# First block of a two-block network on one core: filter spectra moved among the modulation tiles, other modulation kinds moved later, GpSimd arithmetic moved to VectorE, hyena yields made finer

## The chip, the cores and the metric

One core of one Trainium2 chip runs the whole program in one launch. The metric is the device time of one execution in microseconds (us); smaller is better. Five engines work side by side, each through its own queue in order: PE (TensorE: matmuls and transposes), DVE (VectorE), ACT (ScalarE), POOL (GpSimd) and SP, which here only issues transfers from HBM. Float32 weights are used as a pair "high + low" of reduced-precision halves, so that one product takes three matmuls.

## The reference, cut to what matters

The network has two blocks on 256 tokens of width 1024. Only the mixer of the first block is touched:

```python
ada_x = jnp.split(s_lat @ w_ada[l] + b_ada[l], 6, axis=-1)      # six "kinds" of modulation
hx = modulate(rmsnorm(x, norm_mix_g[l]), ada_x[0], ada_x[1])    # kinds 0 and 1
yx, _ = token_mixer(hx, *mix_params, rows, GRID_W, ctx_state)
x = x + ada_x[2][:, None, :] * yx                               # kind 2
hx2 = modulate(rmsnorm(x, norm_ffn_g[l]), ada_x[3], ada_x[4])   # kinds 3 and 4
x = x + ada_x[5][:, None, :] * expert_choice_ffn(...)           # kind 5

def token_mixer(h, ...):
    p = h @ w_in + b_in
    y_a = hyena_branch(p[..., :ML_START], ...)    # 3 projections of 512; z = x_n * longconv(z, filter_n), twice
    y_b, state = mlstm_branch(...)                # q, k, v, o and gates; q, k, v of the context too
    g_a, g_b = jnp.split(jax.nn.sigmoid(p[..., MERGE_START:]), 2, axis=-1)
    return (g_a * (y_a @ w_branch_hy) + g_b * (y_b @ w_branch_ml)) @ w_out, state
```

The two filters of the hyena branch come from a small network of the position (two sines, then `f_w3`, times a decay); a long convolution is a product of spectra.

## The kernel before, in words

`phase_a` writes the first block's mixer, `experts` the expert network, `phase_c` the second block. The order on each engine is laid down at compile time by a list planner: an instruction written earlier has the higher priority, an estimated cost says when it is ready, and ready instructions of lower priority fill gaps. So each engine's order is fixed, but is not the order of the source, and what is late on the chip blocks what stands behind it on its engine. Generators (`filters`, `ada_rest`, `hyena`, `gates`) are advanced with `next` to spread their work over the projections.

**Weights.** Every tile of 1 MB is loaded by SP into one of four `raw` buffers, and `half` turns each of its two halves into high (ACT, line 258) and low (a subtraction, line 259, on DVE or on the engine that `sub` names) in one of four `whl` buffers. `fm` then multiplies (line 255, "mm" tiles in the trace).

**Modulation.** Kinds 0 and 1 are needed first: `ada_tile` loads eight 1 MB tiles and runs four small matmuls on each (line 392). In this loop PE's order is forced to be the order written (`chained`). `ada_close` adds the bias and transposes. The other kinds (`ada_rest`, order 3, 4, 2, 5) take four steps each: one 1 MB tile into a `raw` buffer and two passes over 128x1024 on DVE (lines 423, 425); the last step of a kind adds small matmuls with `ones`.

**Filters.** `filters` yields eight times: after each sine (1, 2), after each half of the two parities (3 to 6; after 4 and 6 the sums and differences `sd` of lines 514, 515), and after each of two spectra `K` in tiles G and H (7, 8), which need the transform table FT from `filter_loads(2)`. Here five steps are taken by the end of tile 3 of the modulation, 6 and 7 after the first hyena projection, 8 after the second.

**Then**: `modT` transposes and modulates x (tiles C, D); six hyena tiles `w_hy`, each followed by `conv` (two DVE passes, lines 618, 619, per 128 columns); in between `modT` of the context (E, F); `hyena` with a spectrum, products with K (lines 808 to 813), sums (816 to 819) and an inverse, twice; gates; `w_k`, `w_v`, `w_q`, `w_o`, and the mLSTM among the eight merge tiles `w_mg`; then `w_br`, `w_out` and the router. The sixteen steps of `ada_rest` go with the last four `w_hy`, the two each of `w_k`, `w_v`, `w_q`, `w_o`, and the first four `w_mg`. The expert weights go through a ring of 18 buffers, filled in order as the mixer frees them; the second round begins when the first expert has used the first.

Of the kernel before, what the change touches and what calls it, by code (L numbers as in the profile page):

```python
# [16 lines left out]
P = 128  # L17
# [210 lines left out]
class Builder:  # L228
# [253 lines left out]
    def filters(self):  # L482

        nc, I, ap = self.nc, self.I, self.ap
        zT, w1, w2, w3, dec, sk = self.fl
        h1, h2 = self.Q[:64, 3, :T], self.Q[:, 3, T:]
        ps = self.psum()
        self.mm(ps[:64, :T], w1, zT, True, True)
        self.sin(h1, ps[:64, :T], self.pfc("fb1")[:64])
        yield  # L490
        ps = self.psum()
        self.mm(ps[:, :T], w2, h1, True, True)
        self.sin(h2, ps[:, :T], self.pfc("fb2"))
        yield

        sd = [self.tl(ap, [P, 2, 2, 512], tag=x) for x in "EF"]
        hv = h2.rearrange("r (m two) -> r two m", two=2)
        for par in range(2):
            h = {}
            for di in range(2):  # L500
                ps = [self.psum(), self.psum()]
                for o in range(2):
                    r = slice(64 * o, 64 * o + 64)
                    self.mm(ps[o], hv[r, par], w3[r, di * 512:(di + 1) * 512], True, True)
                for o in range(2):
                    h[o, di] = self.tl(ap, [P, 512], tag="m2")
                    nc.vector.tensor_mul(h[o, di], ps[o], dec[:, par])
                if di == 0:
                    yield
            for o in range(2):  # L510
                if par == 0:
                    nc.vector.tensor_add(h[o, 0][0:1, :], h[o, 0][0:1, :], sk[:, o])
                    nc.vector.memset(h[o, 1][0:1, :], 0.0)
                nc.gpsimd.tensor_add(sd[o][:, 0, par], h[o, 0], h[o, 1])
                nc.gpsimd.tensor_sub(sd[o][:, 1, par], h[o, 1], h[o, 0])
            yield
        self.K = []
        for o in range(2):
            K = self.tl(ap, [P, 2, 2, 512], tag="GH"[o])
            self.spectrum(K, lambda ri, par: sd[o][:, ri, par])  # L520
            self.K.append(K)
            yield
# [275 lines left out]
    def hyena(self, z0, p1, p2):  # L798

        nc, ap = self.nc, self.ap  # L800
        z = z0
        for o in range(2):
            K = self.K[o]
            U = self.Q.rearrange("p (r s) n -> p r s n", r=2)
            self.spectrum(U, lambda ri, par: z[:, par])
            Y = self.tl(ap, [P, 2, 2, 512], tag="A")
            m = [self.op[:, :1024].rearrange("p (s n) -> p s n", s=2), self.tl(ap, [P, 2, 512], tag="S")]
            nc.vector.tensor_mul(Y[:, 0], U[:, 0], K[:, 0])
            nc.vector.tensor_mul(m[0], U[:, 1], K[:, 1])
            nc.gpsimd.tensor_add(Y[:, 0], Y[:, 0], m[0])  # L810
            nc.vector.tensor_mul(Y[:, 1], U[:, 0], K[:, 1])
            nc.vector.tensor_mul(m[1], U[:, 1], K[:, 0])
            nc.vector.tensor_sub(Y[:, 1], Y[:, 1], m[1])

            Z = U
            nc.vector.tensor_sub(Z[:, 0, 1], Y[:, 1, 0], Y[:, 1, 1])
            nc.vector.tensor_add(Z[:, 1, 1], Y[:, 1, 0], Y[:, 1, 1])
            nc.vector.tensor_add(Z[:, 0, 0], Y[:, 0, 0], Y[:, 0, 1])
            nc.vector.tensor_sub(Z[:, 1, 0], Y[:, 0, 0], Y[:, 0, 1])
            yield  # L820
            if o == 0:
                z = p1
                for par in range(2):
                    ps = self.psum()
                    for ri in (1, 0):
                        self.mm(ps, self.idft[:, par, ri], Z[:, par, ri], ri == 1, ri == 0)
                    nc.vector.tensor_mul(z[:, par], ps, p1[:, par])
            else:
                yy = self.tl(ap, [P, 2, 4, T], F32R, tag="G")
                yh, yl = yy[:, 0], yy[:, 1]  # L830
                for c in range(4):
                    ps = self.psum()
                    for par in range(2):
                        for ri in (1, 0):
                            self.mm(ps[:, par * P:(par + 1) * P], Z[:, par, ri, c * P:(c + 1) * P], self.idft[:, par, ri], ri == 1, ri == 0)
                    y = self.tl(ap, [P, T], tag="s1")
                    by = lambda v: v.rearrange("p (m two) -> p two m", two=2)
                    nc.vector.tensor_mul(by(y), ps[:, :T].rearrange("p (two m) -> p two m", two=2), by(p2[:, c]))
                    self.split(y, yh[:, c], yl[:, c])
                self.ya = yh, yl  # L840
# [10 lines left out]
    def phase_a(self):  # L851
        nc, tc, I = self.nc, self.tc, self.I
        with ExitStack() as es:
# [16 lines left out]
            with self.chained(mybir.EngineType.PE):  # L870
                for kc in range(KC):
                    if kc == 5:
                        xn = self.normed(I["x"], "A")
                    self.ada_tile(kc)
                    if kc == 0:
                        self.filter_loads(1)
                    if kc < 4:
                        next(fil)
            hy = [self.weights(I["w_hy"][0])]
            self.filter_loads(2)  # L880
            cn = self.normed(I["ctx"], "B")
            fm0 = self.ada_close()
            self.iota = self.tl(ap, [P, 32], tag="iota")
            nc.scalar.dma_start(self.iota, I["t_iota"])
# [6 lines left out]
            pfc = self.pfc  # L891
            taps = lambda nm, j, n: [pfc(nm, i * n + j) for i in range(3)]

            parts = []
            zt = self.tl(ap, [P, 2, 2, 512], tag="B")
            z8 = self.tl(self.cst, [P, 2, 4, T], tag="X")
            for p_ in range(3):
                z = z8[:, p_] if p_ < 2 else self.op[:, 1032:2056].rearrange("p (c n) -> p c n", c=4)
                for j in range(2):
                    w = hy.pop() if hy else self.weights(I["w_hy"][2 * p_ + j], sub=(None, nc.gpsimd))  # L900
                    if p_ > 0:
                        next(rest)
                    for c in range(2):
                        n = 2 * j + c
                        ps = self.psum("mm")
                        self.fm(ps[:, :T], w, c, xT)
                        self.conv(z[:, n], ps[:, :T], pfc("b_hy", 4 * p_ + n), taps("hyw", 4 * p_ + n, 12), 4)
                if p_ < 2:
                    next(fil)
                if p_ == 0:  # L910
                    next(fil)
                if p_ == 0:
                    cT = self.modT(cn, gs[:, 1], fm0[:, 1, 0:8], "EF", nc.gpsimd)
                parts.append(self.to_tm(z, zt[:, p_]) if p_ < 2 else z)
            hyena = self.hyena(*parts)
            next(hyena)
            gates = self.gates(xT, cT)
            next(gates)
            qo = self.tl(self.cst, [P, 2, 4, T], tag="X")
# [1 line left out]
            k = self.tl(ap, [P, 4, T], tag="J")  # L921
            kc = q
            for j in range(2):
                w = self.weights(I["w_k"][j], sub=(None, nc.gpsimd))
                next(rest)
                for c in range(2):
                    ps = self.psum("mm")
                    self.fm(ps[:, :T], w, c, cT)
                    self.fm(ps[:, T:], w, c, xT)
                    n = 2 * j + c  # L930
                    self.conv(kc[:, n], ps[:, :T], pfc("b_k", n), taps("mlw", 4 + n, 8), 1, AF.Silu)
                    self.conv(k[:, n], ps[:, T:], pfc("b_k", n), taps("mlw", 4 + n, 8), 4, AF.Silu)
                next(hyena, None)
                next(gates)
            ya = self.ya
            bv = self.tl(ap, [P, 512], tag="m2")
# [3 lines left out]
            for a in (v, vc):  # L940
                nc.gpsimd.memset(a[:, :, :, 128:129], 1.0)
            for j in range(2):
                w = self.weights(I["w_v"][j], sub=(None, nc.gpsimd))
                next(rest)
                for a, src in ((vc, cT), (v, xT)):
                    ps = self.mm2()
# [5 lines left out]
            C0 = self.mlstm_state(kc, vc)  # L952
            self.dump("C0", C0)
            for j in range(2):
                w = self.weights(I["w_q"][j], sub=(None, nc.gpsimd))
                next(rest)
                for c in range(2):
                    n = 2 * j + c
                    ps = self.psum("mm")
                    self.fm(ps[:, :T], w, c, xT)  # L960
                    self.conv(q[:, n], ps[:, :T], pfc("b_q", n), taps("mlw", n, 8), 4, AF.Silu)
            for j in range(2):
                w = self.weights(I["w_o"][j], sub=(None, nc.gpsimd))
                next(rest)
                for c in range(2):
                    n = 2 * j + c
# [10 lines left out]
            rows = self.bias_rows()  # L977
            for j in range(8):
                w = self.weights(I["w_mg"][j])
                if j < 4:  # L980
                    next(rest)
                elif j % 2 == 0:
                    next(rows)
                for c in range(2):
                    n = 2 * j + c
# [752 lines left out]
```

## Time and profile before

| | |
|---|---|
| median of 3 runs | 2452.0 us (2451.36 to 2458.77) |
| profiled execution, its own time | 2461.75 us |
| its span, first to last instruction | 2460.0 us |
| PE / DVE / ACT / POOL busy | 2092.1 / 1003.3 / 734.4 / 90.9 us |
| share of the critical chain, PE / DMA / DVE | 52% / 39% / 6% |

Times within the trace are counted from the span's start. The mixer of the first block takes the first 370 us, the experts go on to about 1240 us, the second block takes the rest. In a timeline the columns are start, duration, engine, line, operation, tiles (written <- read), shapes, count; what stands in brackets is the idle time of the engine just before and what ended it.

### The profile page before, as it was taken

Reading aid. Unit: us, or ns where it says so; the run is one execution under the profiler, and the core shown is the slowest. Engines: PE = TensorE matmul, PEld = TensorE weight load, DVE = VectorE, ACT = ScalarE, POOL = GpSimd, SP = SyncE. Lnnn points to the kernel's source line nnn. Section 1 sums busy time; section 2 is a strip of 40 time slices with the busy share of each in tenths; the row PEclk is TensorE's granted clock in tenths of the full one; section 3 lists DMA queues with packets and bytes.
Section 4 is the critical chain, followed back from the end, with each engine's and each line's share of the span. In section 5 each row is a group of like instructions: output and inputs, shape, how many; then the busy total and the mean of one; then the engine's idle time right before and its main releaser. Section 6 shows DMA issues by size and latency. Waiting matters only on the chain.

```text
span 2460.0 us, 35219 instructions
## 1 busy us (share of the span) xinstructions
PE 2092.1 (85%) x15084; PEld 1515.0 (62%) x15084; DVE 1003.3 (41%) x1494; ACT 734.4 (30%) x1110; POOL 90.9 (4%) x82
## 2 busy tenths in 40 slices
PE   6889987686667666766668999999999999999998
PEld 3778882021111101110117999999999999999998
DVE  5886660000000000000005666656555566657555
ACT  3435631000000000000003644444443554444442
POOL 3321000000000000000000000000000000000000
PEclk8989989798779877987778999999999999999999
DMA  8536579999999999999997445555555545555553
GB/s 309 196 126 221 210 280 378 421 420 420 421 420 421 421 420 421 421 420 421 420 404 262 165 145 177 184 189 187 181 199 194 170 143 179 168 195 181 192 178 107
DMA packets 109079, 675.73 MB, mean 275 GB/s; under 512 B 12245, under 2 KB 20534, under 8 KB 35323
## 3 DMA queue, kind: packets, MB, share of 16 engines
q1 hardware_dynamic: 97226, 657.20, 69.4%
q10 hardware_dynamic: 9952, 10.24, 1.5%
q0 software_dynamic: 1744, 6.04, 0.8%
q8 instruction: 118, 1.93, 0.3%
q14 instruction: 39, 0.31, 0.0%
HBM read 672.36 MB, written 1.08 MB: 274 GB/s over the span
## 4 chain that ended last, share of the span: by engine, by line
PE 52%; DMA 39%; DVE 6%; ACT 1%; issue 1%; POOL 1%; SPq 0%; POOLq 0%; ACTq 0%; DVEq 0%
PE mm L255 46%; DMA raw<-in_w_e 8%; DMA whl<-in_w_e 7%; PE ax L255 4%; DMA A<-in_w_e 2%; DMA acc<-in_w_e 2%; DMA F<-in_w_e 2%; DMA B<-in_w_e 2%; DMA OP<-in_w_e 2%; DMA C<-in_w_e 2%; DMA Q<-in_w_e 2%; DMA H<-in_w_e 2%; PE ax L252 2%; DMA V<-in_w_e 1%; DMA FT<-in_w_e 1%; DMA G<-in_w_e 1%
## 5 line engine op out<-in xcount | busy, mean ns | idle before, releaser
L255 PE MATMUL mm<-C,whl 128*128 128x256 f32 (+1 forms) x4072 | 739.1, 282 | 6.9 <-DVE whl L259 6.9
L259 DVE TENSOR_TENSOR whl<-raw,whl 128x1024 fp32r<-128x1024 f32 (+2 forms) x410 | 494.6, 1210 | 373.3 <-ACT whl L258 372.0
L255 PEld LDWEIGHTS mm<-C,whl 128*128 128x128 f32 (+1 forms) x4072 | 629.0, 189 | 12.8 <-DVE whl L259 7.7
L255 PE MATMUL mm<-D,whl 128*128 128x256 f32 (+1 forms) x2040 | 571.5, 280 | 0.8 <-DVE D L573 0.8
L258 ACT CAST whl<-raw 128x1024 fp32r<-128x1024 f32 (+1 forms) x423 | 435.8, 1035 | 411.6 <-PE mm L255 341.4
L255 PEld LDWEIGHTS mm<-D,whl 128*128 128x128 f32 (+1 forms) x2040 | 384.0, 188 | 4.4 <-issue 3.3
L1188 DVE TENSOR_TENSOR m<-mm,m 128x512 f32<-128x512 f32 x16 | 11.1, 692 | 571.5 <-PE mm L255 571.5
L1187 ACT ACTIVATE m<-mm 128x512 f32<-128x512 f32 x16 | 9.6, 597 | 750.6 <-PE mm L255 750.6
L255 PE MATMUL mm<-whl,C 128*128 128x256 f32 x768 | 141.1, 287 | 1.2 <-ACT whl L258 1.2
L1223 DVE TENSOR_TENSOR S<-mm,J 128x512 f32<-128x512 f32 (+1 forms) x9 | 5.4, 628 | 304.4 <-PE mm L255 304.4
L255 PE MATMUL mm<-raw,N 128*32 128x512 f32 x448 | 86.3, 862 | 46.9 <-DMA raw<-in_w_e 46.9
L255 PE MATMUL mm<-whl,BH 128*128 128x256 f32 x704 | 125.0, 281 | 0.0
L255 PEld LDWEIGHTS mm<-whl,C 128*128 128x128 f32 x768 | 119.6, 192 | 5.5 <-ACT whl L258 2.9
L255 PE MATMUL mm<-whl,N 128*32 128x512 f32 x432 | 73.8, 769 | 44.9 <-DMA whl<-in_w_e 44.8
L255 PE MATMUL mm<-whl,D 128*128 128x256 f32 x384 | 108.7, 283 | 0.0
L255 PEld LDWEIGHTS mm<-whl,BH 128*128 128x128 f32 x704 | 108.0, 188 | 0.0
L255 PE MATMUL mm<-whl,BL 128*128 128x256 f32 x352 | 98.9, 281 | 0.0
L255 PE MATMUL mm<-BH,whl 128*128 128x256 f32 x512 | 91.2, 281 | 0.0
L255 PEld LDWEIGHTS mm<-raw,N 128*32 128x32 f32 x448 | 10.9, 126 | 115.1 <-DMA raw<-in_w_e 108.5
L255 PE MATMUL mm<-whl,E 128*32 128x512 f32 (+2 forms) x304 | 65.8, 580 | 15.9 <-DMA whl<-in_w_e 15.9
L255 PEld LDWEIGHTS mm<-BH,whl 128*128 128x128 f32 x512 | 78.7, 188 | 0.0
L255 PEld LDWEIGHTS mm<-whl,N 128*32 128x32 f32 x432 | 10.1, 120 | 107.2 <-DMA whl<-in_w_e 97.8
(449 smaller groups left out, 2644.2 us busy)
## 6 DMA issues: line engine op xcount, KB each, us to landing
raw<-in_w_e SPq DMA_DIRECT2D x84, 1024.0 KB, 19.8
whl<-in_w_e SPq DMA_DIRECT2D x82, 1024.0 KB, 19.8
raw<-in_w_r SPq DMA_DIRECT2D x48, 1024.0 KB, 5.0
raw<-in_w_gu SPq DMA_DIRECT2D x44, 1024.0 KB, 5.0
raw<-in_w_ada SPq DMA_DIRECT2D x24, 1024.0 KB, 5.4
FT<-in_w_e SPq DMA_DIRECT2D x23, 1024.0 KB, 17.4
Q<-in_w_e SPq DMA_DIRECT2D x23, 1024.0 KB, 17.4
G<-in_w_e SPq DMA_DIRECT2D x23, 1024.0 KB, 17.4
```

The lines of the kernel that those rows point to most:

```text
L252: self.nc.tensor.transpose(dst, src, self.ident[:p, :p])
L255: self.nc.tensor.matmul(dst, l, r, start=a, stop=z)
L258: self.nc.scalar.copy(hi, src)
L259: (sub or self.nc.vector).tensor_sub(lo, src, hi.bitcast(F32))
L1187: nc.scalar.activation(h, pa, AF.Silu)
L1188: nc.vector.tensor_mul(h, pb, h)
L1223: nc.vector.tensor_mul(ye[:, s], py[hf][:, :m], self.a5[:, s])
```

## The change

Five edits, all in the first block:

1. `filters` is advanced in each of the first six modulation tiles (steps 2 to 7, so the first spectrum K is among them) and once more after `modT` of x (step 8). The table FT is loaded after tile 2; the first `w_hy` tile is loaded ahead of modulation tile 7; the context is loaded and normalized after the second `w_hy` tile.
2. The first four `ada_rest` steps leave the hyena projections; all sixteen now go with `w_k`, `w_v`, `w_q`, `w_o` (two each) and all eight `w_mg`.
3. The subtractions of `sd`, the low halves of thirteen weight tiles, the low half of the context's `modT`, and one sum in `hyena` go from POOL to DVE.
4. `hyena` starts after the second projection instead of the third (its last factor is only read at its end), and yields once more, after the first inverse; it is advanced after the `conv`s n = 0, 1 and 3 of `w_k`.
5. The `zt` tile is allocated after the context's `modT`.

```diff
@@ filters, hyena
-                nc.gpsimd.tensor_add(sd[o][:, 0, par], h[o, 0], h[o, 1])
-                nc.gpsimd.tensor_sub(sd[o][:, 1, par], h[o, 1], h[o, 0])
+                nc.vector.tensor_add(sd[o][:, 0, par], h[o, 0], h[o, 1])
+                nc.vector.tensor_sub(sd[o][:, 1, par], h[o, 1], h[o, 0])
...
-            nc.gpsimd.tensor_add(Y[:, 0], Y[:, 0], m[0])
+            nc.vector.tensor_add(Y[:, 0], Y[:, 0], m[0])
...
                     nc.vector.tensor_mul(z[:, par], ps, p1[:, par])
+                yield
@@ phase_a
+                    if kc == 7:
+                        hy = [self.weights(I["w_hy"][0])]
                     self.ada_tile(kc)
                     if kc == 0:
                         self.filter_loads(1)
-                    if kc < 4:
+                    if kc == 2:
+                        self.filter_loads(2)
+                    if kc < 6:
                         next(fil)
-            hy = [self.weights(I["w_hy"][0])]
-            self.filter_loads(2)
-            cn = self.normed(I["ctx"], "B")
...
+            next(fil)
             parts = []
-            zt = self.tl(ap, [P, 2, 2, 512], tag="B")
+            hyena = None
...
-                    w = hy.pop() if hy else self.weights(I["w_hy"][2 * p_ + j], sub=(None, nc.gpsimd))
-                    if p_ > 0:
-                        next(rest)
+                    w = hy.pop() if hy else self.weights(I["w_hy"][2 * p_ + j])
+                    if p_ == 0 and j == 1:
+                        cn = self.normed(I["ctx"], "B")
...
-                if p_ < 2:
-                    next(fil)
                 if p_ == 0:
-                    next(fil)
-                if p_ == 0:
-                    cT = self.modT(cn, gs[:, 1], fm0[:, 1, 0:8], "EF", nc.gpsimd)
+                    cT = self.modT(cn, gs[:, 1], fm0[:, 1, 0:8], "EF", nc.vector)
+                    zt = self.tl(ap, [P, 2, 2, 512], tag="B")
                 parts.append(self.to_tm(z, zt[:, p_]) if p_ < 2 else z)
-            hyena = self.hyena(*parts)
-            next(hyena)
+                if p_ == 1:
+                    parts.append(self.op[:, 1032:2056].rearrange("p (c n) -> p c n", c=4))
+                    hyena = self.hyena(*parts)
+                    next(hyena)
...
-                w = self.weights(I["w_k"][j], sub=(None, nc.gpsimd))
+                w = self.weights(I["w_k"][j])
...
-                next(hyena, None)
+                    if n != 2:
+                        next(hyena, None)
...
                 w = self.weights(I["w_mg"][j])
-                if j < 4:
-                    next(rest)
-                elif j % 2 == 0:
+                next(rest)
+                if j in (4, 6):
                     next(rows)
```

`w_v`, `w_q` and `w_o` lose `sub=(None, nc.gpsimd)` in the same way as `w_k`.

## Rows read from the trace of the kernel before

**Rows 1.** Busy time by stretch: PE, PEld, DVE, ACT, POOL (instructions), granted clock, DMA share, GB/s.
```profile
0.00:33.60 33.60, 19.27 (x80) 3.48 (x80) 13.72 (x32) 4.63 (x8) 7.09 (x13) 0.88 0.93 362
33.60:55.80 22.20, 13.68 (x78) 11.37 (x78) 16.59 (x21) 13.48 (x22) 9.76 (x6) 0.81 0.61 247
55.80:108.60 52.80, 44.29 (x300) 39.67 (x301) 45.81 (x52) 24.51 (x45) 20.35 (x10) 0.90 0.61 200
108.60:160.00 51.40, 45.10 (x284) 36.19 (x284) 47.67 (x66) 18.80 (x33) 15.73 (x8) 0.90 0.39 135
195.60:233.70 38.10, 33.73 (x267) 31.61 (x265) 26.06 (x30) 24.63 (x47) 5.09 (x2) 1.00 0.69 231
233.70:290.20 56.50, 54.54 (x391) 49.52 (x392) 35.20 (x93) 34.82 (x88) 2.31 (x3) 0.94 0.53 181
```

**Rows 2.** PE's timeline, 34 to 165 us: the instructions after its longest gaps.
```profile
55.83 0.79 PE L255 MATMUL mm<-C,whl 128*128 128x256 f32 x2 [6.89 <-DVE whl L259]
70.53 0.66 PE L252 MATMUL ax<-ident,B 128*128 128x128 f32 x4 [1.61 <-DVE G L535]
88.31 0.39 PE L252 MATMUL ax<-ident,X 128*128 128x128 f32 x1 [2.96 <-DVE X L619]
93.32 0.70 PE L252 MATMUL ax<-ident,X 128*128 128x128 f32 x2 [3.90 <-DVE X L619]
136.56 2.07 PE L255 MATMUL ax<-B,FT 128*128 128x512 f32 x2 [5.27 <-DVE B L827]
163.88 0.66 PE L252 MATMUL ax<-ident,N 128*128 128x128 f32 x4 [2.96 <-DVE s L838]
```

**Rows 3.** DVE's timeline: the same forms with and without a POOL instruction beside them.
```profile
27.94 1.42 DVE L550 TENSOR_SCALAR A<-A,rs 128x1024 f32<-128x1024 f32 x2 [0.83 <-POOL rs L324]
47.97 4.52 DVE L550 TENSOR_SCALAR B<-B,rs 128x1024 f32<-128x1024 f32 x2 [1.86 <-POOL rs L324]
52.42 3.36 DVE L259 TENSOR_TENSOR whl<-raw,whl 128x1024 fp32r<-128x1024 f32 x1
57.87 1.21 DVE L259 TENSOR_TENSOR whl<-raw,whl 128x1024 fp32r<-128x1024 f32 x1
80.37 1.27 DVE L425 SCALAR_TENSOR_TENSOR acc<-raw,s,acc 128x1024 f32<-128x1024 f32 x1
83.48 3.37 DVE L425 SCALAR_TENSOR_TENSOR acc<-raw,s,acc 128x1024 f32<-128x1024 f32 x1
157.54 2.37 DVE L662 SCALAR_TENSOR_TENSOR wgt<-wgt 128x32 f32<-128x32 f32 x1
```

**Rows 4.** POOL's groups, 20 to 220 us: line, shapes, count; busy us, mean ns.
```profile
L259 POOL TENSOR_TENSOR whl<-raw,whl 128x1024 fp32r<-128x1024 f32 x13 | 33.9, 2612 | 82.2 <-ACT whl L258 82.2
L573 POOL TENSOR_TENSOR F<-m,E 128x512 fp32r<-128x512 f32 x4 | 7.3, 1842 | 0.0
```

**Rows 5.** PE's timeline: the last modulation tile, and the two spectra K.
```profile
26.65 1.94 PE L392 MATMUL mm<-raw,s 128*32 128x512 f32 x8 [3.24 <-DMA raw<-in_w_ada]
31.62 1.94 PE L392 MATMUL mm<-raw,s 128*32 128x512 f32 x8 [0.55 <-DMA raw<-in_w_ada]
81.53 3.59 PE L255 MATMUL ax<-F,FT 128*128 128x512 f32 x8
```

**Rows 6.** DVE's timeline: small tiles, the halves of the first hyena tile, a wait for DMA.
```profile
38.21 2.35 DVE L259 TENSOR_TENSOR whl<-raw,whl 128x1024 fp32r<-128x1024 f32 x2
66.06 0.68 DVE L533 TENSOR_TENSOR G<-ax,G 128x512 f32<-128x512 f32 x1
102.52 0.74 DVE L423 TENSOR_SCALAR acc<-raw,s 128x1024 f32<-128x1024 f32 x1
201.85 2.61 DVE L425 SCALAR_TENSOR_TENSOR acc<-raw,s,acc 128x1024 f32<-128x1024 f32 x2 [8.49 <-DMA raw<-in_w_ada]
```

**Rows 7.** SP's timeline: the last loads of the expert ring's first round, the first of its second.
```profile
354.72 0.96 SPq L1154 DMA_DIRECT2D whl<-in_w_e  x2
373.21 0.33 SPq L1154 DMA_DIRECT2D acc<-in_w_e  x1
```

More of the change, by code (lines that the diff above doesn't have):

```diff
@@ L942, in phase_a @@
             for j in range(2):
-                w = self.weights(I["w_v"][j], sub=(None, nc.gpsimd))
+                w = self.weights(I["w_v"][j])
                 next(rest)
@@ L954, in phase_a @@
             for j in range(2):
-                w = self.weights(I["w_q"][j], sub=(None, nc.gpsimd))
+                w = self.weights(I["w_q"][j])
                 next(rest)
@@ L962, in phase_a @@
             for j in range(2):
-                w = self.weights(I["w_o"][j], sub=(None, nc.gpsimd))
+                w = self.weights(I["w_o"][j])
                 next(rest)
```

## The prediction, made before the changed kernel was run

> **What bounds the kernel now.** I read the page first: PE 85% busy, and a chain that is PE and DMA. Such shares mix stages, so I went to the busy time by stretch [rows 1]. The edits touch the mixer of the first block, and what they save there is worth its full time: the expert ring's first round is issued by 355.7 us and its second starts at 373.21 [rows 7], when the first expert runs. Its buffers come free as the mixer proceeds, so experts and second block start when the mixer ends, and all behind it shifts with it.
>
> From 33.6 to 160 us [rows 1] PE is busy 13.68 + 44.29 + 45.10 = 103.1 of 126.4 us, and granted 0.81 to 0.90 of its clock, that is, partly its lower level of 1.2 GHz. The same rows give DVE 16.59 + 45.81 + 47.67 = 110.1 us. DVE is the fuller engine here, and each long gap of PE [rows 2] ends on a DVE instruction: a low weight half, a spectrum sum, a `conv`, a hyena product, an output product. So the stage is bound by DVE's queue.
>
> DVE is also slow there for a reason that shows in its rows. The same instruction takes 1.21 or 3.36 us, 1.27 or 3.37, and a pair of 1.42 becomes 4.52 [rows 3]. The long ones run beside a 128x1024 or 128x512 instruction of POOL, which itself takes 1.8 to 2.6 us [rows 4]. I went through DVE's timeline in this stretch: 17 instructions are stretched by over 0.3 us, from the pair at 47.97 to the one at 157.54 [rows 3], by 26.6 us in all.
>
> **The change part by part.**
>
> *POOL's arithmetic to DVE.* It takes the 26.6 us of stretching off DVE in this stretch. It adds nine low halves at 1.21 us [rows 3] (thirteen in all [rows 4], four of them later), four `modT` halves at 0.68 [rows 6] and two hyena sums at 1.21: 10.9 + 2.7 + 2.4 = 16.0 us. The filter sums, eight at 0.68 = 5.4 us, fall before 33.6 us, where DVE is busy 13.72 of 33.6 [rows 1].
>
> *Four `ada_rest` steps out of the hyena projections.* One pass at 0.74 and seven at 1.27 [rows 6, 3]: 9.6 us off DVE here, and four 1 MB loads off SP's queue.
>
> *Filter steps and the first hyena tile forward.* The first spectrum (four sums, 2.7 us), two last filter products (1.4 us) and the halves of the first hyena tile (2.35 us [rows 6]) leave the stretch: 6.4 us.
>
> DVE's load becomes 110.1 - 26.6 + 16.0 - 9.6 - 6.4 = 83.5 us. PE's need is 103.1 us less the slow clock, (1 - 0.81) x 13.68 + 0.10 x 44.29 + 0.10 x 45.10 = 11.5 us, less one spectrum of 3.6 us [rows 5]: 88.0 us. PE would be the bound, and the ceiling of the gain is 126.4 - 88.0 = 38 us. The two loads are close and neither queue will be full throughout, so I price by gap:
>
> - The 6.89 us gap [rows 2] ends on a low half stuck behind the context's normalization (4.52 us) and stretched itself (3.36). The context now comes later and nothing stretches either. Next in line is the same half at its own speed, and PE then still has the first tile's matmuls to run. Gone: 6.9.
> - 1.61, 2.96 and 3.90 us [rows 2] end on a spectrum sum that moves forward, and on `conv`s behind stretched `ada_rest` passes that move away (3.37 at 83.48 [rows 3]). Gone: 8.5.
> - 5.27 and 2.96 us [rows 2] end on hyena and output products behind stretched passes, but two `ada_rest` steps stay in this place and the chain from spectrum to product stays. Half: 4.1.
> - Of the slow clock's 11.5 us, which follows these gaps, under half: 5.0.
> - One spectrum of 3.6 us [rows 5] goes into the modulation loop, where PE waits for tiles: 3.6.
>
> Together 28.1 us. Against it:
>
> - **The front.** In the loop PE keeps the written order, and tile 7's transfer now stands behind 1 MB of `w_hy` and 0.5 MB of FT on SP's queue. Tiles arrive (31.62 - 26.65) / 2 = 2.48 us apart [rows 5] (the first and the last of three tiles), so it lands 1.5 x 2.48 = 3.7 us later. The filter sums and the spectrum must be done on DVE before PE gets to tiles 6 and 7; I find room for them while these tiles land. In return the first hyena tile's halves (2.35 us on DVE) no longer stand inside `modT` of x. The second spectrum's four sums (2.7 us) may stand there, half of them covered: 3.7 - 2.35 + 1.4 = 2.8 us lost. The bounds: 0, if the halves and transposes hide it all, and 8, if both spectra run on PE at the lower clock ahead of tile 7 (twice the 3.6 us of rows 5) and little is returned.
> - **Bursts.** `hyena` now starts after the second projection: six products at 1.21 and eight sums at 0.68 (12.7 us) stand on DVE among the `conv`s and halves of the third, while PE has two tiles. Between 0 (the halves were made ahead) and 12.7 (none of it covered); nearer to the covered end, since four buffers hold two tiles ahead: 5.
> - **The merge stage.** 9.6 us of passes and four loads enter 233.7 to 290.2 us. DVE has 35.2 of 56.5 us there, DMA a share of 0.53, PE is busy 54.54 [rows 1], so there is cover. The passes stand before mLSTM steps and low halves, and each `ada_rest` tile takes one of four `raw` buffers, so SP runs two merge tiles ahead instead of four. Between 0 and 34 (below), nearer to 0 because PE has matmuls of both kinds there: 3.
> - **From 160 to 234 us** four low halves are added (4.8 us) and about as much stretching goes: nothing. The moved context and the `zt` tile cost nothing while the context is needed only for `w_k`, whose cover is four hyena tiles.
>
> Sum: 28.1 - 2.8 - 5 - 3 = 17.3 us. The profiled execution would go from 2461.75 to about 2444; it lies 9.75 us above the median of the runs, so I forecast 2452 - 17 = **2435 us**.
>
> **A rule that speaks against it.** Rows 1 show DVE at 110.1 of 126.4 us and POOL at 9.76 + 20.35 + 15.73 = 45.8 us: the fuller engine takes over the emptier one's work. The Trainium skill, "Perfetto Trace Analysis", section "Optimizing Scalar/DVE Operations", says that with a saturated DVE it can pay to hand operations to other engines, GpSimd included; it adds that GpSimd and DVE share a read port, so that it might not help between those two. Without the second half the sum would be no gain at all; the pairs in rows 3 bear out the second half, 3.36 against 1.21 us, and the sum goes by them.
>
> **The rivals.**
>
> *Faster still.* The hyena chain's gaps go whole (+4.1), the clock recovers fully (+6.5) and the bursts are covered (+5): 33 us, 2419. For it: PE's need of 88 us against 126. Against it: DVE at 83.5 has little slack.
>
> *No change: DVE stays full.* If what stretches DVE is not POOL but the queue itself, DVE's load is 110.1 + 16.0 - 9.6 - 6.4 = 110.1, as before. Or the front takes 8 and the bursts 12.7: 28.1 - 8 - 12.7 - 3 = 4.4 us left. 2448 to 2452. Against the first speaks that short and long rows of one form alternate [rows 3]; for the second, that PE's forced order makes each late sum delay all of the modulation.
>
> *Slower: a DVE pass waits for its load in the merge stage.* DVE waited 8.49 us for an `ada_rest` tile at 201.85 [rows 6]; whatever stands behind such a pass, low halves and mLSTM steps, waits too. If each of the four added steps did so and PE had nothing left, that is 4 x 8.5 = 34 us against 28.1 - 2.8 - 5 = 20.3: 13.7 us slower, 2466. It turns the result slower from 5.1 us of uncovered wait for each step. Against it: in 195.6 to 233.7, with that wait of 8.49 us, PE was idle 38.1 - 33.73 = 4.4 us in all [rows 1], so most was covered.
>
> *It doesn't do what it says.* The mixer gets shorter, but the ring is not full when the first expert runs. From 355.7 to 373.21 [rows 7] no load is issued, and the last three need some 2.5 us each to land, so about 10 us of gain are safe even if loads did not move at all: 2442. They do move, as their buffers come free by the same work. Small, and inside the range.
>
> **How the numbers follow.** Forecast, a gain of 8 to 27 us: 0.63 (with the last rival, 0.05). Faster still: 0.11. No change: 0.16. Slower: 0.10. About 0.3%, 7.4 us, is what a measurement of this kernel can tell from no change. So faster 0.74, same 0.16, slower 0.10. The range reaches from near the faster rival to beyond no change, 2420 to 2455; it leaves out most of the slower case and the end of the faster one.
>
> **What would show it.** Right: DVE passes over 128x1024 at 1.2 to 1.3 us throughout; the gaps of 6.89, 2.96 and 3.90 us gone; the third hyena projection's matmuls done 15 us or more earlier than 108 us; the modulation's last tile 3 to 4 us later than 31.62; the second round of the expert ring near 356 instead of 373.21. Wrong: PE gaps within the modulation loop that end on a `sd` sum; gaps between 233 and 290 us that end on an `acc` pass or on `raw<-in_w_ada`; a DVE that is as busy as before.

## The result: 2428.9 us, and the profile after

The median went from 2455.4 us (four runs beside it) to 2428.9 us; the ratio is 0.9889, with a 95% interval of 0.9862 to 0.9917. That is some 27 us, 20 to 34 by the interval, where 17 were forecast; 2435 was the forecast time and 2420 to 2455 its range.

First I look at where the mixer ends. SP's timeline of the changed kernel, the end of the expert ring's first round and the start of its second:

```profile
318.20 0.33 SPq L1156 DMA_DIRECT2D whl<-in_w_e  x1
323.86 1.64 SPq L1156 DMA_DIRECT2D whl<-in_w_e  x3
342.85 0.33 SPq L1156 DMA_DIRECT2D acc<-in_w_e  x1
```

The second round starts at 342.85 instead of 373.21 [rows 7]: 30.4 us earlier. The two profiled executions are 35.1 us apart (2461.75 and 2426.64), so 4.7 us lie behind the mixer, in stages that the change doesn't touch; runs of the kernel before differ by more than that among themselves. So the mixer is the place.

To split it I take the last output of each stage as a mark: the modulation's bias sum on DVE (line 398), the last `conv` scaling of the third hyena projection, the last SiLU of `w_k`, the last copy of the mLSTM state, the last `w_o` and `w_mg` outputs (all on ACT), and the second ring round. Busy time between the marks, of the kernel before and then of the changed one (columns as in rows 1):

```profile
33.62:109.51 75.89, 58.88 (x380) 51.44 (x381) 63.31 (x72) 38.91 (x68) 31.02 (x16) 0.87 0.60 212
109.51:164.31 54.80, 45.54 (x293) 36.93 (x291) 51.07 (x79) 20.82 (x40) 15.83 (x9) 0.91 0.39 131
164.31:199.39 35.08, 34.74 (x272) 34.11 (x270) 22.46 (x40) 14.61 (x37) 5.24 (x3) 0.90 0.50 175
199.39:222.30 22.91, 22.91 (x185) 21.94 (x184) 15.32 (x16) 14.07 (x24) 5.09 (x2) 1.00 0.57 196
222.30:301.22 78.92, 72.67 (x516) 63.90 (x515) 54.29 (x120) 46.49 (x107) 4.19 (x5) 0.96 0.61 212
301.22:373.21 71.99, 62.08 (x496) 59.31 (x498) 45.85 (x111) 31.27 (x57) 0.71 (x1) 0.91 0.72 274
```

```profile
0.00:36.99 36.99, 22.07 (x92) 5.23 (x92) 23.80 (x48) 7.69 (x12) 2.14 (x9) 0.99 0.95 373
36.99:89.32 52.33, 49.91 (x356) 45.08 (x356) 45.77 (x72) 37.16 (x66) 2.31 (x2) 0.94 0.48 176
89.32:135.65 46.33, 42.70 (x300) 37.45 (x301) 42.23 (x80) 20.80 (x39) 1.30 (x3) 0.93 0.52 180
135.65:167.52 31.87, 30.98 (x250) 30.20 (x249) 23.95 (x40) 13.38 (x36) 0.11 (x1) 0.95 0.54 179
167.52:191.45 23.93, 23.93 (x205) 23.92 (x204) 17.63 (x23) 14.50 (x25) 0.00 (x0) 1.00 0.67 236
191.45:270.77 79.32, 74.11 (x523) 64.50 (x522) 58.53 (x124) 46.42 (x106) 4.18 (x5) 0.98 0.65 233
270.77:342.85 72.08, 61.87 (x493) 59.12 (x495) 46.89 (x112) 31.46 (x58) 0.71 (x1) 0.91 0.76 297
```

The hyena projections take 52.3 instead of 75.9 us, `w_k` with its hyena chain 46.3 instead of 54.8. From the bias sum to the last `w_k` output, PE was busy 104.4 of 130.7 us before and is busy 92.6 of 98.7 now; DVE 114.4 before, 88.0 now. PE has become the fuller engine, as the forecast said. The later stages are as long as before within 3.2 us.

DVE's timeline of the changed kernel, the forms of [rows 3]:

```profile
52.51 0.75 DVE L550 TENSOR_SCALAR B<-B,rs 128x1024 f32<-128x1024 f32 x1 [0.21 <-POOL rs L324]
68.23 1.22 DVE L259 TENSOR_TENSOR whl<-raw,whl 128x1024 fp32r<-128x1024 f32 x1
76.45 1.27 DVE L425 SCALAR_TENSOR_TENSOR acc<-raw,s,acc 128x1024 f32<-128x1024 f32 x1
```

In the whole mixer no DVE instruction is stretched by over 0.3 us any more. PE's timeline, the instructions after its gaps of over 1.5 us between 33 and 320 us:

```profile
34.67 1.06 PE L392 MATMUL mm<-raw,s 128*32 128x512 f32 x8 [1.76 <-DMA raw<-in_w_ada]
37.93 1.09 PE L252 MATMUL ax<-ident,g 128*128 128x128 f32 x4 [2.20 <-DVE g L398]
92.84 0.39 PE L255 MATMUL mm<-C,whl 128*32 128x256 f32 x1 [4.87 <-DVE whl L259]
261.64 0.69 PE L255 MATMUL mm<-C,whl 128*128 128x256 f32 x2 [3.86 <-DVE whl L259]
```

All six gaps of [rows 2] are gone. The first two rows are the front's price (the bias sum had 0.91 us of gap behind it before, 2.20 now), the third the burst of hyena products, the fourth the merge stage's passes: the three costs that the forecast named, each with a gap. Of its other signs, the last output of the third hyena projection comes 20.2 us earlier, and the second round of the ring earlier than the 356 us forecast.

### The profile page after: what moved, and what is told of

Read it like the earlier page. It is cut to its first block, busy times and chain, and to the rows that moved or that the text cites. A ratio compares the mean times of both kernels' runs of the same rounds, so it can differ in the third digit from the quotient of the medians.

```text
span 2424.9 us, 35211 instructions
## 1 busy us (share of the span) xinstructions
PE 2086.1 (86%) x15084; PEld 1502.8 (62%) x15084; DVE 996.2 (41%) x1521; ACT 734.7 (30%) x1110; POOL 32.5 (1%) x55
## 3 DMA queue, kind: packets, MB, share of 16 engines
HBM read 672.36 MB, written 1.08 MB: 278 GB/s over the span
## 4 chain that ended last, share of the span: by engine, by line
PE 53%; DMA 40%; DVE 5%; ACT 1%; issue 1%; POOL 0%; SPq 0%; POOLq 0%; ACTq 0%; DVEq 0%
PE mm L255 47%; DMA whl<-in_w_e 8%; DMA raw<-in_w_e 8%; PE ax L255 4%; DMA A<-in_w_e 3%; DMA B<-in_w_e 2%; DMA Q<-in_w_e 2%; DMA OP<-in_w_e 2%; DMA G<-in_w_e 2%; DMA C<-in_w_e 2%; DMA H<-in_w_e 2%; PE ax L252 2%; DMA acc<-in_w_e 2%; DMA F<-in_w_e 2%; DMA FT<-in_w_e 1%; DMA V<-in_w_e 1%
## 5 line engine op out<-in xcount | busy, mean ns | idle before, releaser
L259 DVE TENSOR_TENSOR whl<-raw,whl 128x1024 fp32r<-128x1024 f32 (+1 forms) x423 | 508.3, 1206 | 370.4 <-ACT whl L258 368.9
L255 PEld LDWEIGHTS mm<-BH,whl 128*128 128x128 f32 x512 | 78.1, 188 | 0.0
```

The lines of the kernel that those rows point to most:

```text
L255: self.nc.tensor.matmul(dst, l, r, start=a, stop=z)
L259: (sub or self.nc.vector).tensor_sub(lo, src, hi.bitcast(F32))
```

## The experiments

Theory A: POOL's instructions stretch those of DVE beside them, DVE's queue sets the pace, and this is most of the gain. Theory B: the four modulation steps moved out of the full stretch are most of it. Others follow from these. All ratios are to runs of the kernel before on the same chip.

### One part alone, and one part undone

**e1_pool_only**: the kernel before with edit 3 alone.

```diff
-                nc.gpsimd.tensor_add(sd[o][:, 0, par], h[o, 0], h[o, 1])
+                nc.vector.tensor_add(sd[o][:, 0, par], h[o, 0], h[o, 1])
...
-                w = self.weights(I["w_k"][j], sub=(None, nc.gpsimd))
+                w = self.weights(I["w_k"][j])
```

> The kernel before with edit 3 alone: POOL's arithmetic goes to DVE, all else stays in its old place. Theory A (POOL's instructions beside DVE's stretch these, and that is most of what the change removes): DVE's load between 33.6 and 160 us falls by 26.6 - 16.0 = 10.6 us, the gap of 6.89 us goes and the ones of 2.96 and 3.90 us shrink; 10 to 18 us faster than before. Theory B (what counts is the four modulation steps moved out of DVE's full stretch, not who does the arithmetic): DVE stays full, within 5 us of before. The 128x1024 passes on DVE take 1.2 to 1.3 us throughout by theory A.

Measured: 2435.5 us, ratio 0.9912 (0.9893 to 0.9931): 21.6 us. More than theory A's own 10 to 18, and no support for B. (Theory A's 10.6 us left out four filter sums, 2.7 us, that stay in this stretch without edit 1.) No DVE instruction is stretched and the six gaps of [rows 2] are gone, but PE's timeline has two others between 33 and 165 us, on a low half and on a modulation pass (in e12_pool_only_again, below, they are 3.07 and 5.17 us as well):

```profile
83.95 0.51 PE L255 MATMUL mm<-C,whl 128*128 128x256 f32 x2 [3.07 <-DVE whl L259]
151.10 3.54 PE L255 MATMUL ax<-ones,acc 128*128 128x1 f32 x16 [5.17 <-DVE acc L425]
```

**e2_keep_pool**: the changed kernel with edit 3 undone.

> The changed kernel with edit 3 undone: POOL keeps its arithmetic, all moves stay. Theory A: 12 to 20 us of the 27 are lost, DVE shows passes of 2.5 to 3.4 us again. Theory B: at most 5 us are lost.

Measured: 2443.7 us, ratio 0.9954 (0.9935 to 0.9972). About 16 of the 27 us are lost, as theory A expected. The stretched instructions are back, as DVE's timeline shows, here on a `conv` and on a sum of hyena:

```profile
55.64 2.63 DVE L619 SCALAR_TENSOR_TENSOR X<-s,pf,X 128x252 f32<-128x252 f32 x1
95.53 2.85 DVE L819 TENSOR_TENSOR Q<-A 128x512 f32<-128x512 f32 x1
```

So the moves are worth 11 us as long as POOL still works beside DVE, and about 5 once it doesn't.

**e3_rest_only**: the kernel before with edit 2 alone.

```diff
-                    if p_ > 0:
-                        next(rest)
...
-                if j < 4:
-                    next(rest)
-                elif j % 2 == 0:
+                next(rest)
+                if j in (4, 6):
                     next(rows)
```

> The kernel before with edit 2 alone: the first four modulation steps leave the hyena projections, all sixteen go with later tiles. Theory A: 9.6 us of DVE passes go, but stretching stays; 3 to 8 us faster. Theory B: 10 us or more faster. If the merge stage pays for the steps (the slower rival), it is no faster than before.

Measured: 2455.7 us, ratio 0.999 (0.9975 to 1.0006): a difference that can't be told from none. Theory B falls, A's own 3 to 8 us don't show either, and the third case, that the merge stage pays, is what came. The marks show why: the last hyena output comes 5.2 us earlier than before (104.27) and the last `w_k` output 6.4 (157.93), but the merge stage takes 84.4 us instead of 78.9. What was won is given back there.

**e4_rest_back**: the changed kernel with edit 2 undone.

> The changed kernel with edit 2 undone: four modulation steps are back among the hyena projections. Theory A: 3 to 8 us lost. Theory B: 10 us or more lost. If the later place costs in the merge stage as much as the earlier one did, nothing is lost and the gap of 3.86 us at 261.64 goes.

Measured: 2432.0 us, ratio 0.9901 (0.9882 to 0.9919); some 3 us are lost, which the intervals don't tell from none. Theory B falls here too, and the gap of 3.86 us is gone, as the third case expected. Its merge stage takes 72.6 us (79.3 in the changed kernel), and its stages from `w_k` to `w_o` some 8 us more; one modulation pass with its closing matmuls shows in PE's timeline:

```profile
95.25 3.55 PE L255 MATMUL ax<-ones,acc 128*128 128x1 f32 x16 [6.48 <-DVE acc L425]
```

### Is it the stretching?

The same can be tested without taking work off POOL's results: leave the changed kernel as it is and let POOL do something that nobody reads.

**e5_twice**: after DVE's low half, POOL does the same subtraction again into the used raw buffer, for thirteen tiles. DVE's order stays that of the changed kernel (in the trace all but three instructions, from 163 us on).

```diff
+    def extra(self, raw, w):
+        lo = raw[:, 1024:]
+        self.nc.gpsimd.tensor_sub(lo, lo, w[1][0].bitcast(F32))
```

> The changed kernel, and POOL does the low half's subtraction of thirteen weight tiles once more, in place in the raw buffer, after DVE's own; nobody reads the result. DVE does all that it does in the changed kernel, in the same order, and nothing waits for POOL except the next load into that raw buffer, some 2.5 us later. Theory A (POOL's instructions stretch DVE's, and DVE's queue sets the pace): thirteen stretches of about 2 us come back, DVE shows passes of 2.5 to 3.4 us, and 8 to 20 us of the 27 are lost. Rival A2 (POOL's arithmetic cost time because its result came late, 2.6 us instead of 1.2 us): at most 4 us are lost.

Measured: 2453.3 us, ratio 0.9984 (0.9971 to 0.9998). Nearly the whole gain is gone, more than theory A expected, though DVE does all it does in the changed kernel and no DVE instruction reads what POOL writes. DVE's timeline shows why: twelve of the thirteen subtractions each stretch one DVE instruction, by 21.0 us in all.

**e9_hold**: the control. The same buffers are held about as long, but POOL only writes zeros. The list planner lays DVE's order out anew for it; some forty of 330 instructions up to the merge stage stand in another place than in the changed kernel.

```diff
-        self.nc.gpsimd.tensor_sub(lo, lo, w[1][0].bitcast(F32))
+        self.nc.gpsimd.memset(lo, 0.0); self.nc.gpsimd.memset(lo, 0.0); self.nc.gpsimd.memset(lo, 0.0)
```

> As the kernel with the subtraction done twice (e5_twice, which lost 24 of the 27 us), but POOL only writes zeros three times into the same half of the raw buffer. The buffer is held about as long, POOL is busy about as long, but it reads no operand. If e5_twice lost its time because the raw buffers came free later, this loses 15 us or more too. If it lost it because POOL's instructions with two operands stretch DVE's, this loses at most 6 us and DVE's 128x1024 passes stay at 1.2 to 1.3 us. If any POOL instruction stretches DVE's, DVE's long passes are back here too.

Measured: 2429.6 us, ratio 0.9885 (0.9861 to 0.9909): nothing is lost. Busy time of both from 33.6 to 235 us, and the groups of POOL's extra work and of two DVE passes (count; busy us, mean ns), first e5_twice:

```profile
33.60:235.00 201.40, 176.12 (x1282) 159.96 (x1281) 170.89 (x250) 102.28 (x197) 39.63 (x19) 0.93 0.52 184
L285 POOL TENSOR_TENSOR raw<-raw,whl 128x1024 f32<-128x1024 f32 x13 | 36.8, 2832 | 97.3 <-DVE whl L259 88.6 <-issue 4.4 <-ACT s L620 3.5
L432 DVE SCALAR_TENSOR_TENSOR acc<-raw,s,acc 128x1024 f32<-128x1024 f32 x21 | 34.2, 1630 | 12.2 <-DMA raw<-in_w_ada 12.1
L626 DVE SCALAR_TENSOR_TENSOR X<-s,pf,X 128x252 f32<-128x252 f32 x8 | 7.5, 934 | 0.1
```

and e9_hold:

```profile
33.60:235.00 201.40, 190.72 (x1412) 172.74 (x1411) 164.93 (x288) 114.93 (x237) 41.32 (x45) 0.95 0.56 196
L285 POOL MEMSET raw<- 128x1024 f32 x39 | 38.2, 980 | 82.3 <-DVE whl L259 62.5 <-issue 17.9 <-DVE rv L329 0.5
L432 DVE SCALAR_TENSOR_TENSOR acc<-raw,s,acc 128x1024 f32<-128x1024 f32 x21 | 26.9, 1279 | 1.1 <-DMA raw<-in_w_ada 0.9
L626 DVE SCALAR_TENSOR_TENSOR X<-s,pf,X 128x252 f32<-128x252 f32 x8 | 3.8, 475 | 0.2
```

POOL is busy as long in both (36.8 and 38.2 us of extra work). In e5_twice the modulation pass takes 1630 ns in the mean of 21, of which four are stretched, to 2.3 to 3.5 us, and the `conv` pass 934 in the mean of eight, of which two are, to 2.1 and 2.5. With the zeros they take 1279 and 475, as in the changed kernel, and none is stretched. PE's busy time in the stretch falls from 190.7 to 176.1 us in e5_twice. In the hyena projections 8.6 us of stretching lie in a stage that takes 62.0 us instead of the 53.0 of e9_hold and the 52.3 of the changed kernel, whose DVE order it shares there. So it isn't the time at which POOL's results came, nor the hold on the buffers by itself: in this stage stretched DVE instructions are the cause, and this is shown.

A part of the loss comes by a longer way. The merge stage takes 84.5 us in e5_twice and 78.1 in e9_hold, though POOL computes nothing beside DVE there. In e5_twice PE waits 5.2 us in it for an mLSTM product (`qs`) on DVE that stands behind modulation passes. DVE comes late to it, and its rows show one reason: it waited 7.66 us up to 188.98 for a load that SP issued at 183.59, when POOL had just let go of the raw buffer (its subtraction ran from 180.21 to 183.56). In e9_hold loads wait for POOL too, but DVE waits 0.9 us in all for them, in its other order. For these 6.4 us the runs don't separate the stretching from the hold.

### The moves

**e6_hyena_back**: the changed kernel with edit 4 undone.

> The changed kernel with edit 4 undone: hyena starts after the third projection, in the old steps. If the burst of products that ends in the 4.87 us gap at 92.84 costs what the gap is long, this is 0 to 5 us faster than the changed kernel. If the earlier start pays for itself by shortening the chain of spectra behind w_k, it is 3 to 10 us slower.

Measured: 2428.8 us, ratio 0.9883 (0.9861 to 0.9905), as the changed kernel. The 4.87 us gap is gone, the last hyena and `w_k` outputs come 3.5 and 7.2 us earlier (85.83, 128.47), but the state is copied at 168.03 instead of 167.52: gaps of 1.8 to 2.1 us behind the gates take its place. The result sits at the lower end of the first expectation, zero, and misses the second; the order of hyena doesn't matter to the sum.

**e7_filters_back**: the changed kernel with edit 1 undone.

> The changed kernel with edit 1 undone: filter steps 6 to 8, the table and the context's load back in their old places. By the sum of the prediction this part gives 3.6 us (one spectrum into the wait for tiles) plus 1.6 us (the gap on a spectrum sum) and 2.7 us of DVE's load, less 2.8 us at the front: 2 to 7 us are lost. If the later close of the modulation (36.99 instead of 33.62 us) outweighs what is gained, it is faster than the changed kernel.

Measured: 2430.4 us, ratio 0.9889 (0.9869 to 0.9909): no loss that can be measured, where 2 to 7 us were expected. The bias sum is back at 32.94 us, the last hyena output is 2.8 us later than in the changed kernel, the last `w_k` output 2.9 us earlier and the state 1.5 us later: the front's loss and the stage's gain nearly cancel, and PE waits 4.07 us behind the gates, at 148.16, where the changed kernel has no gap over 1.4. Beside e11_again (below), which is the changed kernel on the same chip, it is 3 us slower, within the intervals.

**e8_rest_at_kv**: two modulation steps at each `w_k` and `w_v` tile, four in the merge stage.

> The changed kernel, with two modulation steps instead of one at each w_k and w_v tile, and so only four in the merge stage, as before. PE has twice the matmuls on these tiles. If the merge stage pays for its four added steps (79.3 us from the last w_o output to the last merge output in the changed kernel, 72.6 us with four steps fewer), 4 to 7 us are won there, and the result is 2 to 7 us faster than the changed kernel. If the two steps at w_k only move the cost to DVE's full stretch, it is within 3 us of it or slower.

Measured: 2433.1 us, ratio 0.9899 (0.9879 to 0.9919), not faster. The merge stage is 74.4 us, 4.9 less, but from the last `w_k` output to the state it takes 41.4 instead of 31.9 us; 7.1 us of it are a gap of PE behind the gates, at 154.25. The cost moves with the steps.

**e10_pool_and_rest**, **e11_again**, **e12_pool_only_again**: the kernel before with edits 2 and 3; the changed kernel; edit 3 alone; all on one chip.

> The kernel before with edits 2 and 3, without the filters' and hyena's moves (1, 4, 5). Theory: edit 3 gives 22 us, edit 2 some 3 more, edits 1 and 4 nothing once DVE is no longer stretched: within 4 us of the changed kernel. If edits 1 and 4 do matter when both are missing, it is 5 us or more behind the changed kernel.

> The changed kernel once more, on the same chip as the two beside it: 25 to 29 us faster than before.

> Edit 3 alone once more, on the same chip as the changed kernel: 20 to 23 us faster than before, that is 4 to 7 us behind the changed kernel. If edit 3 is all there is, within 2 us of it.

Measured: 2429.8 us, ratio 0.9889 (0.9863 to 0.9915); 2427.0, 0.9876 (0.9853 to 0.9899); 2430.8, 0.9896 (0.9869 to 0.9924). The three lie within 4 us and their intervals overlap. By the ratio the changed kernel is a little above its expected 25 to 29 us, and edit 3 alone above its 20 to 23. Edits 1, 4 and 5 add some 3 us to 2 and 3, not told from none. Edit 3 alone gave 22 us in its first runs and, by the ratio, 26 in these; the full change 27 and 30. What the moves add to it is 4 to 6 us, near what these runs can resolve. No variant was clearly faster than the changed kernel.

## Why the prediction was right, step by step

**The place and the bound: right.** The mixer ends 30.4 us earlier and what follows shifts with it; the last rival (ring not full) didn't come about, since the last loads of the first round are issued at 325.5, 17 us ahead of the second.

**POOL's arithmetic to DVE: right, and the main part.** The stretching of 26.6 us is gone, the added passes run at their own speed, and e5_twice with e9_hold shows that the stretching costs time. But DVE's load alone isn't the gain: in e1_pool_only DVE's busy time up to the second ring round falls by only 8.3 us (266.0 to 257.7), while that round comes 26.9 us earlier. PE's idle time falls by 18.7 us (57.1 to 38.4), since it no longer waits at stretched instructions, and its busy time by 8.2, at a granted clock of 0.95 instead of 0.91. To price by gap, and not by DVE's load, was the right step. The Trainium skill, "Perfetto Trace Analysis", section "Optimizing Scalar/DVE Operations", read by its first half (hand work to other engines where DVE is saturated), would have given no gain; its warning about the port that GpSimd and DVE share agrees with the trace, 1630 against 1279 ns.

**The terms, by stage.** The forecast's terms are put to the stage in which they fall, and the clock's 5.0 us by the slow clock of rows 1 (3.0 and 2.0):

| stage, up to its last output | forecast | measured (from the profiles) |
|---|---|---|
| front and hyena projections: 6.9 + 8.5 + 3.6 + 3.0 - 2.8 | 19.2 us | 109.51 - 89.32 = 20.2 us |
| `w_k` and the hyena chain: 4.1 + 2.0 - 5 | 1.1 us | 54.80 - 46.33 = 8.5 us |
| `w_v`, state, `w_q`, `w_o` | 0 | 3.2 - 1.0 = 2.2 us |
| merge stage | -3 | 78.92 - 79.32 = -0.4 us |
| `w_br`, `w_out`, router | 0 | -0.1 us |
| sum | 17.3 us | 30.4 us |

The first line is nearly exact partly by luck. The prediction puts the burst (5) among the third projection's `conv`s, that is, in this line; the table has it in the second, since 3.5 of the 4.87 us of its gap fall behind the mark at 89.32. As predicted, the two lines would read 14.2 against 20.2 and 6.1 against 8.5. In the front the last modulation tile came 3.05 us later (34.67 instead of 31.62), against 3.7 worked out, and the bias sum 3.4 us later, against 2.8 for the front as a whole. The slow clock, summed as in the prediction over the first two lines, cost 0.13 x 58.88 + 0.09 x 45.54 = 11.8 us before and 0.06 x 49.91 + 0.07 x 42.70 = 6.0 after: 5.8 us back (an estimate), 5.0 forecast.

**Mis-sized: the gaps of 5.27 and 2.96 us.** I counted half of them, since two modulation steps and the chain of spectra stay in this place. They went whole, and the granted clock of the stage, 0.91 before, is 0.93 even with the new gap of 4.87 us in it. The burst itself was sized right: 5 us forecast, 4.87 us of gap. By rows, PE is idle 46.33 - 42.70 = 3.6 us there instead of 54.80 - 45.54 = 9.3.

**Mis-sized: the merge stage, twice, and the errors cancel.** Without the added steps (e1_pool_only, e4_rest_back, e12_pool_only_again) the stage takes 72.3 to 72.7 us (74.4 in e8_rest_at_kv), with them (the changed kernel, e6, e7, e10, e11) 78.3 to 79.9: the four steps cost about 6.5 us (5 by e8_rest_at_kv), not 3. But removing POOL's work shortens the stage by 6.3 us (78.9 to 72.6), which I had put at nothing "from 160 to 234 us". What goes is this gap, at the border of the prediction's two stretches, and the granted clock of the stage rises from 0.96 to 1.00:

```profile
233.66 0.80 PE L255 MATMUL ax<-OP,qs 128*128 128x129 f32 x2 [4.29 <-DVE qs L757]
```

The rows of [rows 2] end at 165 us and don't show it. It is nearly all of the 4.4 us of idle PE that I read between 195.6 and 233.7 as proof that the wait of 8.49 us was covered; the product stands behind two modulation passes, at 230.33. Where POOL computes among the projections, PE waits there (2.9 us in e3_rest_only, 3.6 in e2_keep_pool, 5.2 in e5_twice); in e1_pool_only and the changed kernel it waits 0.5 us or less. In e3_rest_only, without that help, the steps cost 84.4 - 78.9 = 5.5 us and use up the gain of the move.

**The slower rival** named the right place. Its mechanism was there in small: each of the four steps cost about 1.6 us, under the 5.1 us from which it would have decided, and the 3.86 us gap ends on a low half that stands behind modulation passes. The waits for loads are the smaller part: in this stage DVE waits 2.1 us for them in the changed kernel and 1.1 in e4_rest_back, while it is busy 58.5 instead of 50.3 us.

**Faster still** came near, though only in part by its own conditions: the mixer is 30.4 us shorter, where that rival had 33. The hyena chain's gaps did go whole; the clock did not recover fully (0.94 and 0.93) and the burst was not covered. What came beyond the forecast came in part from stages where none was forecast: 2.2 us from `w_v` to `w_o` and 2.6 in the merge stage.

**Parts that I credited and that gave nothing of their own.** The first spectrum's move into the modulation loop (3.6 us) and edit 1 as a whole: e7_filters_back loses 0 or 3 us, by which run of the changed kernel it is put beside, and neither can be told from none. It was right that the spectrum hides there, but PE is the fuller engine afterwards, and the front's 3.4 us take it back. In the same way edit 2 is worth some 3 us (e4_rest_back), not told from none, and edit 4 nothing (e6_hyena_back). The gaps that I shared out among the edits were all due to one of them: with edit 3 alone the six close. Two others, of 3.07 and 5.17 us, open in their place; with edit 2 beside it (e10_pool_and_rest) they go, and the merge stage pays.

## What to carry to other kernels

Before handing elementwise work to GpSimd, compare rows of one VectorE form with and without a GpSimd instruction beside it; if they differ, the hand-over can cost the fuller engine more than the work itself would (26.6 us of stretching against 16.0 here). When several edits aim at the same idle time, price each one with the others in place: their gains don't add up, and the first that fills the fuller engine takes most. A step moved out of a full stage has to be charged where it lands (5 to 7 us for four steps here, as much as it freed).

## What the runs showed of the hardware

By the rows a stretched DVE instruction waits; it does not run slower. In e5_twice a stretched modulation pass ends 1.08 us after the POOL subtraction beside it and a stretched `conv` pass 0.28 us after it, whenever they began. It goes the other way too: a POOL subtraction that meets a DVE low half, which takes its usual 1.21 us, takes 3.60 us, where the shortest take 2.4 to 2.6:

```profile
193.40 2.58 POOL L285 TENSOR_TENSOR raw<-raw,whl 128x1024 f32<-128x1024 f32 x1 [9.84 <-DVE whl L259]
193.63 3.43 DVE L432 SCALAR_TENSOR_TENSOR acc<-raw,s,acc 128x1024 f32<-128x1024 f32 x1
58.42 3.60 POOL L285 TENSOR_TENSOR raw<-raw,whl 128x1024 f32<-128x1024 f32 x1 [3.50 <-ACT s L620]
58.61 1.21 DVE L259 TENSOR_TENSOR whl<-raw,whl 128x1024 fp32r<-128x1024 f32 x1
```

What POOL does matters. Its subtractions of two 128x1024 operands stretch two-operand DVE instructions (modulation pass 1279 to 1630 ns in the mean of 21, `conv` pass 475 to 934 in the mean of 8), while zeros written by POOL over the same bytes leave both as they are. The two differ in what POOL reads and in the length of one instruction (2.83 and 0.98 us), which no run here separates. The one-operand pass over the context is another matter: where no POOL instruction runs beside it, in e5_twice, it took 751 ns in the mean of two (the first line below), and beside the zeros of e9_hold 1275 (the second).

```profile
L557 DVE TENSOR_SCALAR B<-B,rs 128x1024 f32<-128x1024 f32 x2 | 1.5, 751 | 0.6 <-POOL rs L331 0.6
```

```profile
L557 DVE TENSOR_SCALAR B<-B,rs 128x1024 f32<-128x1024 f32 x2 | 2.5, 1275 | 0.2 <-POOL rs L331 0.2
```

The Trainium skill, "SBUF — State Buffer", section "SBUF: two separate sides", states a rule that fits: DVE and GpSimd share one pair of ports, held by one instruction at a time; a DVE instruction with two SBUF inputs competes for it only with a GpSimd instruction that reads SBUF, one in a two-port mode with any. The first half agrees with 1279 against 1630 ns; the second would explain 751 against 1275, though no run here shows which mode that pass was in.

How much a kernel pays for this was not expected either: thirteen POOL subtractions, 36.8 us of work whose results nothing reads, cost 2453.3 - 2429.6 = 23.7 us against about the same time spent on zeros, in part by the loads that wait for the raw buffers.
